# Gate and up products of a SwiGLU in seven half-width products per chunk instead of eight

## The chip, the core and the metric

The kernel runs on one core of a Trainium2 chip. The metric is the device time of one execution in microseconds (us); the profile is one execution on the same chip. The engines are named as the profile names them: PE does the matmuls, PEld loads their weights, DVE is the vector engine, ACT the scalar engine, POOL the GpSimd engine, SP issues the DMAs.

## The reference, cut to what is computed

Four SwiGLU feed-forward networks (FFN 0 to 3 below) stand in a trunk of two layers, one ahead of and one behind each mixer; the mixers are a causal pooling layer and a latent attention layer. T = 512 tokens, D = 1024, F = 2816, all in float32.

```python
def swiglu(u, wg, wu, wd):
    return (jax.nn.silu(u @ wg) * (u @ wu)) @ wd

for l in range(DEPTH):
    h = h + 0.5 * swiglu(rmsnorm(h, ffn_pre_norm[l]), ffn_pre_wg[l], ffn_pre_wu[l], ffn_pre_wd[l])
    u = rmsnorm(h, mix_norm[l])
...
    h = h + 0.5 * swiglu(rmsnorm(h, ffn_post_norm[l]), ffn_post_wg[l], ffn_post_wu[l], ffn_post_wd[l])
...
return rmsnorm(h, final_norm)
```

## The kernel before

The residual h lies transposed in SBUF, as eight tiles h0 to h7 of 128 features by 512 tokens. Float32 precision is kept by splitting every operand into a rounded high part and a low part; `mm3` (L84) makes each product of three matmuls, high by high, high by low and low by high (L86 to L88). The high part of a weight tile is a cast on ACT (L118), the low part a subtraction on DVE (L119); a weight tile is 128 x 1024 (512 KB) and comes by one DMA into the ring `wraw` of four.

F is cut into 22 chunks of 128. In an FFN, `rms` sums the squares over the features with eight pairs of one-column matmuls (`token_sums`, L156), takes the root on DVE (`rsqrt`, twelve small operations, L167 to L174) and `on_all` spreads the result to all partitions (a product on DVE called `diag`, L197, a matmul, L204, a copy on ACT called `rb`). The norm is applied behind the gate and up products, so these can start before it is known: the gained, unnormalised h, split into `gh_hi` and `gh_lo`, is their moving operand.

Chunks 0 and 1 are computed together, k by k as h arrives (96 matmuls). Each further chunk takes 48 matmuls of 512 columns, 24 for the gate and 24 for the up product; `gated` (L280) then multiplies by rb on DVE, takes the silu on ACT, multiplies gate and up on POOL (L287) and splits the product into `mh` and `ml`. The down product runs twice per FFN, behind chunk 10 and behind chunk 21: `down` (L317) sums 11 chunks into a PSUM tile for each of the eight d and DVE adds it to h (L324). In the last FFN d = 6 and 7 of the second time go by halves of the tokens, so that the first half of the output can be finished early.

A tile scheduler orders the instructions of each engine from its own estimates. PSUM has a ring of six tiles `mm` and of two tiles `aux`.

Of the kernel before, what the change touches and what calls it, by code (L numbers as in the profile page):

```python
# [16 lines left out]
P = 128  # L17
T = 512
# [4 lines left out]
NFH = NF // 2  # L23
# [17 lines left out]
def trunk_kernel(  # L41
# [20 lines left out]

    nc = tc.nc
# [11 lines left out]
    def f(ap):  # L75
        return ap.bitcast(F32)
# [7 lines left out]
    def mm3(out, w, x, start, stop):  # L84

        nc.tensor.matmul(out, w[0], x[0], start=start, stop=False)  # L86
        nc.tensor.matmul(out, w[0], x[1], start=False, stop=False)  # L87
        nc.tensor.matmul(out, w[1], x[0], start=False, stop=stop)  # L88
# [11 lines left out]
    more, count = [], [0]  # L100

    def load_w(src, parts=1, loads=1, lo_engines=(nc.vector,), before=None):
# [3 lines left out]
        pools = [wsplit_sb] + more  # L106
        pool = pools[count[0] % len(pools)]
        count[0] += 1
        hi = pool.tile([P, UNIT], F32R, tag="whi", name="whi")
        lo = pool.tile([P, UNIT], F32R, tag="wlo", name="wlo")  # L110
# [16 lines left out]
    room = ExitStack()  # L127
    more.append(room.enter_context(tc.tile_pool(name="wsplit2", bufs=4)))
# [80 lines left out]
    class Norm:  # L209
# [39 lines left out]

        def rb(self, ts=slice(0, T)):  # L250
            return on_all(rms(self.squares, D, (ts.stop - ts.start) // P))
# [23 lines left out]

    def ffn(idx, norm, on_h, first=None, last=False):
        rb = norm.rb()
        with tc.tile_pool(name="mid", bufs=1) as midp, tc.tile_pool(name="act", bufs=2) as actp:

            def gated(j, gate, up):  # L280

                tg = actp.tile([P, T], F32, tag="tg", name="tg")
                tu = actp.tile([P, T], F32, tag="tu", name="tu")
                nc.vector.tensor_tensor(out=tg, in0=gate, in1=rb, op=ALU.mult)  # L284
                nc.scalar.activation(tg, tg, AF.Silu)
                nc.vector.tensor_tensor(out=tu, in0=up, in1=rb, op=ALU.mult)  # L286
                nc.gpsimd.tensor_tensor(out=tu, in0=tu, in1=tg, op=ALU.mult)  # L287
                hi = midp.tile([P, T], F32R, tag=f"mh{j}", name=f"mh{j}")
                lo = midp.tile([P, T], F32R, tag=f"ml{j}", name=f"ml{j}")
                nc.scalar.copy(hi, tu)  # L290
                nc.vector.tensor_tensor(out=lo, in0=tu, in1=f(hi), op=ALU.subtract)  # L291
                return hi, lo

            for half in range(2):
                mid = []
                if half == 0:

                    ps = [mm_tile() for _ in range(4)]
                    for u in range(ND // 2):
                        w = part(first[u] if first is not None else load_w(wfirst[idx, u]), 2, 4, P)  # L300
                        for c in (2 * u, 2 * u + 1):
                            for m in range(4):
                                mm3(ps[m], [x[:, c % 2, m] for x in w], norm.gh[c], c == 0, c == ND - 1)
                    mid += [gated(0, ps[0], ps[1]), gated(1, ps[2], ps[3])]
                for j in range(len(mid), NFH):
                    ps = []
                    for m in range(2):
                        w = part(load_w(wgu[idx, half * NFH + j - 2, m]), ND, P)
                        o = mm_tile()
                        for c in range(ND):  # L310
                            mm3(o, [x[:, c] for x in w], norm.gh[c], c == 0, c == ND - 1)
                        ps.append(o)
                    mid.append(gated(j, *ps))

                units = {}

                def down(d, ts):  # L317
                    o = mm_tile()
                    for j in range(NFH):
                        u, k = divmod(d * NFH + j, 8)  # L320
                        if u not in units:
                            units[u] = part(load_w(wd[idx, half, u]), 8, P)
                        mm3(o[:, ts], [x[:, k] for x in units[u]], [x[:, ts] for x in mid[j]], j == 0, j == NFH - 1)
                    nc.vector.scalar_tensor_tensor(  # L324
                        out=h[d][:, ts], in0=o[:, ts], scalar=0.5, in1=h[d][:, ts], op0=ALU.mult, op1=ALU.add)
                    if half == 1:
                        on_h(d, ts)

                n_whole = ND - 2 if last and half == 1 else ND
                for d in range(n_whole):  # L330
                    down(d, slice(0, T))
                if n_whole < ND:
                    for th in range(2):
                        for d in range(n_whole, ND):
                            down(d, slice(th * T // 2, (th + 1) * T // 2))
# [107 lines left out]
    class Shared:  # L443


        def __init__(self, norm):
            mean = mean_of(token_sums(norm.squares), D)
            self.gh, self.r = norm.gh, on_all(rsqrt(mean, "rms_r"))
            shared_kv(mean, self.r)

        def rb(self):
            return self.r
# [354 lines left out]
```

## Time and profile before

| | us |
|---|---|
| median of 3 runs | 1790.08 (1787.37 to 1966.82) |
| the profiled execution | 1788.47 |
| its span | 1786.7 |
| PE busy | 1758.8 (98%) |
| DVE busy | 843.2 (47%) |
| ACT busy | 629.4 (35%) |
| POOL busy | 316.2 (18%) |

The span is the time from the first to the last instruction that the profiler recorded; the execution's own time is 1.8 us longer. A matmul's recorded duration is longer than its spacing to the next, since matmuls are pipelined: what one costs in a stream is read from start to start. The same holds, by about 0.08 us, for DVE operations that follow each other.

### The profile page before, as it was taken

Reading aid. Unit: us, or ns where it says so; the run is one execution under the profiler, and the core shown is the slowest. Engines: PE = TensorE matmul, PEld = TensorE weight load, DVE = VectorE, ACT = ScalarE, POOL = GpSimd, SP = SyncE. Lnnn points to the kernel's source line nnn. Section 1 sums busy time; section 2 is a strip of 40 time slices with the busy share of each in tenths; the row PEclk is TensorE's granted clock in tenths of the full one; section 3 lists DMA queues with packets and bytes.
Section 4 is the critical chain, followed back from the end, with each engine's and each line's share of the span. In section 5 each row is a group of like instructions: output and inputs, shape, how many; then the busy total and the mean of one; then the engine's idle time right before and its main releaser. Section 6 shows DMA issues by size and latency. Waiting matters only on the chain. (4 is left out here: it accounts for less than half of the span.)

```text
span 1786.7 us, 20848 instructions
## 1 busy us (share of the span) xinstructions
PE 1758.8 (98%) x8238; PEld 1466.5 (82%) x8238; DVE 843.2 (47%) x1248; ACT 629.4 (35%) x948; POOL 316.2 (18%) x192
## 2 busy tenths in 40 slices
PE   8999999999999999999999999999999999999997
PEld 6888888888888888888888888888887888888886
DVE  7443444465433444465434443487675744334433
ACT  5332222353221233333322332376664532222221
POOL 3220022122210121101200222212121222101212
PEclk9999999999999999999999999999999999999998
DMA  7322223222322233223232322221221333222301
GB/s 249 102 98 95 94 96 104 95 85 87 102 95 94 95 100 100 95 87 96 95 96 95 104 95 71 65 69 51 77 84 59 130 100 102 94 95 95 103 27 48
DMA packets 49553, 166.34 MB, mean 93 GB/s; under 512 B 6320, under 2 KB 6320, under 8 KB 49456
## 3 DMA queue, kind: packets, MB, share of 16 engines
q1 hardware_dynamic: 49456, 165.02, 28.3%
q8 instruction: 65, 1.06, 0.3%
q14 instruction: 32, 0.26, 0.0%
HBM read 158.44 MB, written 2.10 MB: 90 GB/s over the span
## 5 line engine op out<-in xcount | busy, mean ns | idle before, releaser
L118 ACT CAST whi<-wraw 128x1024 fp32r<-128x1024 f32 (+2 forms) x332 | 315.4, 959 | 730.8 <-PE mm L87 656.3
L86 PE MATMUL mm<-gh_hi,whi 128*128 128x512 f32 x1424 | 557.2, 391 | 6.6 <-ACT whi L118 6.6
L87 PE MATMUL mm<-gh_lo,whi 128*128 128x512 f32 x1424 | 556.9, 391 | 0.0
L88 PE MATMUL mm<-gh_hi,wlo 128*128 128x512 f32 x1424 | 555.3, 391 | 0.0
L119 DVE TENSOR_TENSOR wlo<-wraw,whi 128x1024 fp32r<-128x1024 f32 (+2 forms) x302 | 372.0, 1233 | 201.2 <-ACT whi L118 200.6
L287 POOL TENSOR_TENSOR tu<-tu,tg 128x512 f32<-128x512 f32 x88 | 192.5, 2188 | 1029.2 <-ACT whi L118 842.7
L86 PEld LDWEIGHTS mm<-gh_hi,whi 128*128 128x128 f32 x1424 | 268.6, 189 | 63.0 <-ACT whi L118 6.6
L88 PEld LDWEIGHTS mm<-gh_hi,wlo 128*128 128x128 f32 x1424 | 268.6, 189 | 56.7 <-issue 0.7
L87 PEld LDWEIGHTS mm<-gh_lo,whi 128*128 128x128 f32 x1424 | 268.7, 189 | 56.3 <-issue 0.5
L86 PE MATMUL mm<-mh,whi 128*128 128x512 f32 (+1 forms) x726 | 277.9, 383 | 0.0
L87 PE MATMUL mm<-ml,whi 128*128 128x512 f32 (+1 forms) x726 | 276.4, 383 | 0.0
L88 PE MATMUL mm<-mh,wlo 128*128 128x512 f32 (+1 forms) x726 | 276.4, 383 | 0.0
L286 DVE TENSOR_TENSOR tu<-mm,rb 128x512 f32<-128x512 f32 x88 | 60.8, 691 | 260.5 <-PE mm L88 260.5
L87 PEld LDWEIGHTS mm<-ml,whi 128*128 128x128 f32 x726 | 136.4, 188 | 26.8
L86 PEld LDWEIGHTS mm<-mh,whi 128*128 128x128 f32 x726 | 136.4, 188 | 26.6
L88 PEld LDWEIGHTS mm<-mh,wlo 128*128 128x128 f32 x726 | 136.4, 188 | 26.5
L291 DVE TENSOR_TENSOR ml<-tu,mh 128x512 fp32r<-128x512 f32 x88 | 63.3, 721 | 131.4 <-ACT mh L290 130.9
L290 ACT CAST mh<-tu 128x512 fp32r<-128x512 f32 x88 | 54.5, 621 | 188.9 <-POOL tu L287 188.2
L324 DVE SCALAR_TENSOR_TENSOR h<-mm,h 128x512 f32<-128x512 f32 (+1 forms) x66 | 44.5, 675 | 143.0 <-PE mm L88 143.0
L284 DVE TENSOR_TENSOR tg<-mm,rb 128x512 f32<-128x512 f32 x88 | 60.8, 691 | 85.7 <-PE mm L88 81.4
L241 POOL TENSOR_TENSOR sq_acc<-sq_acc,sq 128x512 f32<-128x512 f32 (+1 forms) x43 | 60.4, 1405 | 217.7 <-ACT sq L237 217.2
L119 POOL TENSOR_TENSOR wlo<-wraw,whi 128x512 fp32r<-128x512 f32 (+1 forms) x30 | 40.6, 1354 | 195.9 <-ACT whi L118 189.8
(165 smaller groups left out, 1450.4 us busy)
## 6 DMA issues: line engine op xcount, KB each, us to landing
wraw<-in_wgu SPq DMA_DIRECT2D x160, 512.0 KB, 3.3
wraw<-in_wd SPq DMA_DIRECT2D x88, 512.0 KB, 3.3
wraw<-in_wo SPq DMA_DIRECT2D x16, 512.0 KB, 3.4
wraw<-in_wfirst SPq DMA_DIRECT2D x12, 512.0 KB, 3.3
wraw<-in_wheads SPq DMA_DIRECT2D x8, 512.0 KB, 3.3
h<-in_xT SPq DMA_DIRECT2D x8, 256.0 KB, 5.9
wraw<-in_wfirst SPq DMA_DIRECT2D x8, 256.0 KB, 6.0
qr<-yh SPq DMA_DIRECT2D x32, 64.0 KB, 2.0
```

The source lines that it names most:

```text
L86: nc.tensor.matmul(out, w[0], x[0], start=start, stop=False)
L87: nc.tensor.matmul(out, w[0], x[1], start=False, stop=False)
L88: nc.tensor.matmul(out, w[1], x[0], start=False, stop=stop)
L118: nc.scalar.copy(hi[:, s], raw[:, s])
L119: lo_engines[i % len(lo_engines)].tensor_tensor(out=lo[:, s], in0=raw[:, s], in1=f(hi[:, s]), op=ALU.subtract)
L241: nc.gpsimd.tensor_tensor(out=self.acc[:, ts], in0=self.acc[:, ts], in1=self.sq[:, ts], op=ALU.add)
L284: nc.vector.tensor_tensor(out=tg, in0=gate, in1=rb, op=ALU.mult)
L286: nc.vector.tensor_tensor(out=tu, in0=up, in1=rb, op=ALU.mult)
L287: nc.gpsimd.tensor_tensor(out=tu, in0=tu, in1=tg, op=ALU.mult)
L290: nc.scalar.copy(hi, tu)
L291: nc.vector.tensor_tensor(out=lo, in0=tu, in1=f(hi), op=ALU.subtract)
L324: nc.vector.scalar_tensor_tensor(out=h[d][:, ts], in0=o[:, ts], scalar=0.5, in1=h[d][:, ts], op0=ALU.mult, op1=ALU.add)
```

## The change

Chunks 2 to 21 of each FFN compute gate and up by Strassen's algorithm for 2 x 2 blocks. The blocks of the weights are gate and up by the two halves of K; the blocks of the tokens are the two halves of K by the two halves of T. Seven products replace eight, each of 4 k by 3 matmuls of 256 columns: 84 matmuls of 256 columns per chunk in place of 48 of 512. Products p1 to p7 are summed in PSUM and, where they enter more than one result, by ACT copies and DVE sums.

- `group_weights` forms four sums of weight blocks per chunk with POOL additions of 128 x 512 (L165 of the new code) and splits 3.5 tiles of 128 x 1024 (a, half of rb, s13, s24) where the kernel before split two.
- `Quarters` forms the sums of token blocks once per FFN, 24 small DVE operations (those of 256 columns and the splits of `t12`, `t4` and `t3`, L357 to L375) and their casts on ACT.
- The down product goes in six parts of 2, 4, 4, 4, 4 and 4 chunks (`PARTS`). Two d of a part stand behind each chunk of the next part; h is added to six times per d instead of twice (L491).
- The product of gate and up is on DVE rather than POOL.
- PE's order in an FFN is the order of the code (`manual_schedule`): in the first Strassen chunk p1, p2, p6, then `on_all`, then p7 and p5; in a later one p1, p2, p4 of the chunk before, p6, p5, p3 of the chunk before, p7, then the two down products.
- Weight splits have one ring of four pairs; a further ring of four (`wsplit2`, `wsplit3`) is gone, and small pools `wb`, `wf`, `gx` and `act` are new.

```diff
+PARTS = (2, 4, 4, 4, 4, 4)
+    def group_weights(idx, g, wb):
+        ra, rb = (wraw_sb.tile([P, UNIT], F32, tag="wraw", name="wraw") for _ in range(2))
+        nc.sync.dma_start(ra, wgu[idx, g - 2, 0])
+        nc.sync.dma_start(rb, wgu[idx, g - 2, 1])
+        q0, q1, whole = slice(0, 512), slice(512, UNIT), slice(0, UNIT)
+        def add(out, x, y):
+            nc.gpsimd.tensor_tensor(out=out, in0=x, in1=y, op=ALU.add)
+        a = split_w(ra, wsplit_sb, "w")
+        split_into(a, ra, whole)
+        a22 = split_w(rb[:, q0], room.wf, "f")
+        split_into(a22, rb[:, q0], q0)
+        add(rb[:, q0], rb[:, q0], rb[:, q1])
+        add(rb[:, q1], rb[:, q1], ra[:, q0])
+        s13 = split_w(rb, wsplit_sb, "w")
+        split_into(s13, rb, whole)
+        add(ra[:, q0], rb[:, q0], ra[:, q0])
+        add(ra[:, q1], ra[:, q0], ra[:, q1])
+        s24 = split_w(ra, wb, "w")
+        split_into(s24, ra, whole)
...
+            def product(g, to, w, x, start=True):
+                if start:
+                    acc[g][to] = mm_tile()[:, :HT]
+                for k in range(4):
+                    mm3(acc[g][to], weights[g][w](k), quarters.operand(x, k), start and k == 0, k == 3,
+                        skip_group_check=True)
...
+            def p3(g):
+                product(g, "y1", "s4", "b22", start=False)
+                y = acc[g].pop("y1")
+                nc.vector.tensor_tensor(out=y, in0=act[g]["c16"], in1=y, op=ALU.add)
+                gate_half(g, 1, y)
+                gate = act[g]["g"]
+                silu(gate)
+                m = room.act.tile([P, T], F32, tag="m", name="m", bufs=3)
+                nc.vector.tensor_tensor(out=m[:, :HT], in0=acc[g].pop("x"), in1=gate[:, :HT], op=ALU.mult)
+                nc.vector.tensor_tensor(out=m[:, HT:], in0=act[g]["c167"], in1=gate[:, HT:], op=ALU.mult)
+                split_mid(g, m)
...
+                    p1(g)
+                    p2(g)
+                    if before is None:
+                        p6(g)
+                        rb = norm.spread(r)
+                        for j in range(2):
+                            gated(j, ps[2 * j], ps[2 * j + 1])
+                        gate_half(g, 0, acc[g].pop("y2"))
+                        p7(g)
+                        p5(g)
+                        up_half(g)
+                    else:
+                        gate_half(g, 0, acc[g].pop("y2"))
+                        p4(before)
+                        p6(g)
+                        p5(g)
...
+                            p3(before)
+                            p7(g)
+                            up_half(g)
...
+                    if n_part == 0:
+                        todo = [(d, None) for d in ((), (0, 1, 2), (3, 4, 5), (6, 7))[i]]
+                    elif i == 0:
+                        todo = [(d, rest) for d in (0, 1)]
+                    else:
+                        todo = [(d, [n - 1]) for d in (0, 1)] if i == 1 else []
+                        todo += [(2 * i + j, None) for j in range(2)]
```

On PE, the kernel before has `on_all` of FFN 0 (its matmul is L204) among the products of chunks that came ahead of it:

```order
L86 MATMUL mm<-gh_hi,whi 128x512
L87 MATMUL mm<-gh_lo,whi 128x512
L204 MATMUL aux<-diag,ones 128x512
L88 MATMUL mm<-gh_hi,wlo 128x512
L86 MATMUL mm<-gh_hi,whi 128x512
```

In the changed kernel PE has it (L261) behind p6 of chunk 2, with t the summed token blocks:

```order
L91 MATMUL mm<-t_hi,whi 128x256
L92 MATMUL mm<-t_lo,whi 128x256
L93 MATMUL mm<-t_hi,wlo 128x256
L261 MATMUL aux<-diag,ones 128x512
L91 MATMUL mm<-gh_hi,whi 128x256
L92 MATMUL mm<-gh_lo,whi 128x256
```

Ahead of `on_all` of FFN 0 PE now has the token sums, 96 matmuls of 512 columns (chunks 0 and 1) and 36 of 256 (p1, p2 and p6 of chunk 2); before it had the token sums and 110 of 512.

On DVE in FFN 0 before, the last rows ahead of diag are the root's, among weight splits (L119) for chunks ahead:

```order
L172 TENSOR_TENSOR rms_t<-rms_r,mean 128x4
L173 SCALAR_TENSOR_TENSOR rms_t<-rms_t,rms_r 128x4
L119 TENSOR_TENSOR wlo<-wraw,whi 128x1024
L174 SCALAR_TENSOR_TENSOR rms_r<-rms_t,rms_r 128x4
L172 TENSOR_TENSOR rms_t<-rms_r,mean 128x4
L173 SCALAR_TENSOR_TENSOR rms_t<-rms_t,rms_r 128x4
L174 SCALAR_TENSOR_TENSOR rms_r<-rms_t,rms_r 128x4
L197 TENSOR_TENSOR diag<-ident,rms_r 128x512
```

In the changed kernel twelve rows of DVE in the same place begin with the last token sums (t, gh_lo) and the weight splits of chunks 2 and 3 (L153); the root's rows stand between these, and diag (L254) follows eleven rows behind the last one shown:

```order
L362 SCALAR_TENSOR_TENSOR t_416<-h_89,g_neg,t_409 128x256
L375 TENSOR_TENSOR gh_lo<-t_416,gh_hi 128x256
L153 TENSOR_TENSOR wlo<-wraw,whi 128x1024 x2
L375 TENSOR_TENSOR t_lo<-t_409,t_hi 128x512
L239 TENSOR_SCALAR mean<-aux 128x4
L375 TENSOR_TENSOR t_lo<-t_416,t_hi 128x256
L224 TENSOR_SCALAR rms_t<-mean 128x4
L153 TENSOR_TENSOR wlo<-wraw,whi 128x1024
L226 TENSOR_SCALAR rms_r<-rms_t 128x4
L410 TENSOR_TENSOR mm<-c_460,mm 128x256
L153 TENSOR_TENSOR wlo<-wraw,whi 128x1024
L229 TENSOR_TENSOR rms_t<-rms_r,mean 128x4
```

From the first gh_lo to diag DVE has 68 rows in FFN 0, where it had 37; POOL, for which DVE's weight splits wait, has eight additions of weight blocks for these two chunks besides its six sums of squares.

On DVE a chunk in the middle of an FFN was five rows before, two weight splits, tg, tu and ml:

```order
L284 TENSOR_TENSOR tg<-mm,rb 128x512
L119 TENSOR_TENSOR wlo<-wraw,whi 128x1024
L286 TENSOR_TENSOR tu<-mm,rb 128x512
L119 TENSOR_TENSOR wlo<-wraw,whi 128x1024
L291 TENSOR_TENSOR ml_944<-tu,mh_943 128x512
```

It is sixteen rows now, of which twelve stand here; L153 and L119 are weight splits, L410, L432 and L442 sums of products, L416, L455, L447 and L448 the gating, L491 adds to h:

```order
L153 TENSOR_TENSOR flo<-wraw,fhi 128x512
L442 TENSOR_TENSOR mm<-c_1429,mm 128x256
L416 TENSOR_TENSOR gate<-mm,rb 128x256
L153 TENSOR_TENSOR wlo<-wraw,whi 128x1024
L455 TENSOR_TENSOR gate<-gate,rb 128x512
L119 TENSOR_TENSOR wlo<-wraw,whi 128x1024
L432 TENSOR_TENSOR c_1645<-c_1645,mm 128x256
L447 TENSOR_TENSOR m<-mm,gate 128x256
L448 TENSOR_TENSOR m<-c_1479,gate 128x256
L153 TENSOR_TENSOR wlo<-wraw,whi 128x1024
L491 SCALAR_TENSOR_TENSOR h_88<-aux,h_88 128x512
L462 TENSOR_TENSOR ml_1630<-m,mh_1629 128x512
```

The four rows not shown are the split of a, the sum L410, the first half's L416 and the second L491.

## Rows read from the trace of the kernel before

**Rows 1.** Page, part 1: busy us, share of the span and instructions of each engine.
```profile
PE 1758.8 (98%) x8238; PEld 1466.5 (82%) x8238; DVE 843.2 (47%) x1248; ACT 629.4 (35%) x948; POOL 316.2 (18%) x192
```

**Rows 2.** Page, part 5: costliest groups; busy, mean ns | idle before, its releaser.
```profile
L118 ACT CAST whi<-wraw 128x1024 fp32r<-128x1024 f32 (+2 forms) x332 | 315.4, 959 | 730.8 <-PE mm L87 656.3
L86 PE MATMUL mm<-gh_hi,whi 128*128 128x512 f32 x1424 | 557.2, 391 | 6.6 <-ACT whi L118 6.6
```

**Rows 3.** Timeline, PE, 48 matmuls apart: start us, duration us, instruction.
```profile
302.36 0.39 PE L86 MATMUL mm<-gh_hi,whi 128*128 128x512 f32 x1
...
313.24 0.39 PE L86 MATMUL mm<-mh,whi 128*128 128x512 f32 x1
```

**Rows 4.** Timeline, PE, last FFN, 35 matmuls of 256 columns apart.
```profile
1753.95 0.28 PE L86 MATMUL mm<-mh,whi 128*128 128x256 f32 x1
...
1758.15 0.28 PE L88 MATMUL mm<-mh,wlo 128*128 128x256 f32 x1
```

**Rows 5.** Groups by shape, DVE: busy us, mean ns | idle before.
```profile
L264 DVE TENSOR_TENSOR ptl<-aux,pth 128x256 fp32r<-128x256 f32 x16 | 6.7, 416 | 0.6 <-ACT pth L263 0.6
```

**Rows 6.** Timeline, DVE, FFN 0: 128x512 with and without POOL beside it.
```profile
15.97 1.78 DVE L224 SCALAR_TENSOR_TENSOR gh_lo<-h,g_sb,gh_hi 128x512 fp32r<-128x512 f32 x1
17.68 1.78 DVE L119 TENSOR_TENSOR wlo<-wraw,whi 128x512 fp32r<-128x512 f32 x1
19.38 0.74 DVE L224 SCALAR_TENSOR_TENSOR gh_lo<-h,g_sb,gh_hi 128x512 fp32r<-128x512 f32 x1
20.05 0.68 DVE L119 TENSOR_TENSOR wlo<-wraw,whi 128x512 fp32r<-128x512 f32 x1
```

**Rows 7.** Timeline, POOL, FFN 0: one 128x512 addition.
```profile
10.79 1.29 POOL L241 TENSOR_TENSOR sq_acc<-sq_acc,sq 128x512 f32<-128x512 f32 x1 [1.74 <-ACT sq L237]
```

**Rows 8.** Timeline, PE in FFN 0 around the token sums.
```profile
22.05 0.38 PE L156 MATMUL aux<-ones,sq 128*128 128x1 f32 x2 [0.56 <-DVE sq L234]
...
25.49 0.63 PE L87 MATMUL mm<-gh_lo,whi 128*128 128x512 f32 x1
25.91 0.63 PE L88 MATMUL mm<-gh_hi,wlo 128*128 128x512 f32 x1
```

**Rows 9.** Timeline, FFN 0: DVE from its first row to diag, then PE's on_all.
```profile
5.51 0.75 DVE L224 SCALAR_TENSOR_TENSOR gh_lo<-h,g_sb,gh_hi 128x512 fp32r<-128x512 f32 x1 [4.48 <-ACT gh_hi L219]
...
35.94 0.69 DVE L197 TENSOR_TENSOR diag<-ident,rms_r 128x512 f32<-128x512 f32 x1
...
38.07 1.02 PE L204 MATMUL aux<-diag,ones 128*128 128x512 f32 x2
```

**Rows 10.** Timeline, FFN 1: the pooling's h, a weight split, PE's first product.
```profile
389.77 0.74 DVE L385 SCALAR_TENSOR_TENSOR h<-mm,g_sb,h 128x512 f32<-128x512 f32 x1
390.43 1.22 DVE L119 TENSOR_TENSOR wlo<-wraw,whi 128x1024 fp32r<-128x1024 f32 x1
391.56 0.74 DVE L385 SCALAR_TENSOR_TENSOR h<-mm,g_sb,h 128x512 f32<-128x512 f32 x1
...
396.18 0.44 PE L86 MATMUL mm<-gh_hi,whi 128*128 128x512 f32 x1
```

**Rows 11.** Windows, ahead of FFN 3: busy us of PE, PEld, DVE, ACT, POOL, then the clock.
```profile
1392.00:1413.50 21.50, 21.50 (x97) 17.61 (x96) 21.50 (x23) 15.79 (x22) 10.21 (x6) 1.00 0.46 153
```

**Rows 12.** Timeline, DVE, FFN 3: the root's first row and diag.
```profile
1416.20 0.15 DVE L182 TENSOR_SCALAR mean<-aux 128x4 f32<-128x4 f32 x1
...
1418.64 0.69 DVE L197 TENSOR_TENSOR diag<-ident,rms_r 128x512 f32<-128x512 f32 x1
```

**Rows 13.** Page, part 6: a weight tile's DMA, KB and us to landing.
```profile
wraw<-in_wgu SPq DMA_DIRECT2D x160, 512.0 KB, 3.3
```

**Rows 14.** Timeline, the kernel's tail: DVE and POOL.
```profile
1762.60 0.43 DVE L234 TENSOR_TENSOR sq<-h 128x256 f32<-128x256 f32 x1
...
1773.07 5.50 POOL L691 TENSOR_TENSOR y<-hg,rb 128x256 f32<-128x256 f32 x8 [4.06 <-ACT rb L206]
...
1779.40 1.41 DVE L706 TENSOR_SCALAR y<-mm,rms_r 128x512 f32<-128x512 f32 x2
```

More of the change, by code (lines that the diff above doesn't have):

```diff
@@ L22 @@
 NF = F // P
-NFH = NF // 2
+HT = T // 2
+PARTS = (2, 4, 4, 4, 4, 4)
+N_MID = 8
 H = 16
@@ L105, in load_w @@
         raw = wraw_sb.tile([P, UNIT], F32, tag="wraw", name="wraw")
[L106 to L110, printed above, removed]
+        hi = wsplit_sb.tile([P, UNIT], F32R, tag="whi", name="whi")
+        lo = wsplit_sb.tile([P, UNIT], F32R, tag="wlo", name="wlo")
         for i in range(loads):
@@ L248, in add, with r, spread @@
                 step()
+        def r(self, ts=slice(0, T)):
+            return rms(self.squares, D, (ts.stop - ts.start) // P)
+        def spread(self, r):
+            return on_all(r)
         def rb(self, ts=slice(0, T)):
-            return on_all(rms(self.squares, D, (ts.stop - ts.start) // P))
+            return on_all(self.r(ts))
     def split_gain(src, base, c, pool, tag):
@@ L288, in gated @@
                 hi = midp.tile([P, T], F32R, tag=f"mh{j}", name=f"mh{j}")
                 lo = midp.tile([P, T], F32R, tag=f"ml{j}", name=f"ml{j}")
[L290 to L335, printed above, removed]
@@ new lines, in ffn, with down @@
+            blocks, units, o_of = {}, {}, {}
+            whole = slice(0, T)
+            def down(part_of, d, js=None, ts=whole, tile_of=mm_tile):
+                base, n = part_of
+                js = js or range(n)
+                o = o_of.pop(d, None) or tile_of()
+                for j in js:
+                    at = blocks.setdefault((d, base + j), len(blocks))
+                    u, k = divmod(at, 8)
+                    if u not in units:
+                        units[u] = part(load_w(wd[idx, u]), 8, P)
+                    mm3(o[:, ts], [x[:, k] for x in units[u]], [x[:, ts] for x in mids[base + j]], j == 0, j == n - 1)
+                if js[-1] != n - 1:
+                    o_of[d] = o
+                    return
+                nc.vector.scalar_tensor_tensor(
+                    out=h[d][:, ts], in0=o[:, ts], scalar=-0.5, in1=h[d][:, ts], op0=ALU.mult, op1=ALU.add)
+                if base + n == NF:
+                    on_h(d, ts)
@@ L338, in trunk_kernel @@
+            n = PARTS[-1]
+            under = base - n, n
+            for js in (range(n - 1), [n - 1]):
+                for d in range(2):
+                    down(under, d, js)
+            n_whole = ND - 2 if last else ND
+            for d in range(2, n_whole):
+                down(under, d)
+            for th in range(2):
+                for d in range(n_whole, ND):
+                    down(under, d, ts=slice(th * HT, (th + 1) * HT))
     norm = Norm(G_PRE)
@@ L671, in trunk_kernel @@
                     out_proj(dd, [heads[4 * q4 - 4 + k] for k in range(4)], wos, False)
-        for dd in range(ND):
-            if dd % 2 == 0:
-                wos = part(load_w(wo[3, dd // 2], **aw), 2, 4, P)
-            out_proj(dd, [heads[12 + k] for k in range(4)], wos, True)
-    more.append(ctx.enter_context(tc.tile_pool(name="wsplit3", bufs=4)))
+    room.open()
+    for dd in range(ND):
+        if dd % 2 == 0:
+            wos = part(load_w(wo[3, dd // 2], **aw), 2, 4, P)
+        out_proj(dd, [heads[12 + k] for k in range(4)], wos, True)
     norm = nxt
@@ L719, in trunk_kernel @@
     ffn(3, norm, on_h, last=True)
+    room.close()
 def _layout(a):
```

189 lines of the change are left out of this document (163 added, 26 removed).

## The prediction

> **What bounds the kernel now.** I read the page first: PE is busy 98% of the span, DVE 47%, POOL 18% [rows 1]. Then the groups of instructions: the costliest matmul waited 6.6 us in 1786.7, while ACT's weight casts waited 656 us for PE to free their buffers [rows 2]. The weights are ready before PE wants them; nearly every microsecond taken off PE's stream comes off the time, as long as PE is not made to wait. The question is therefore double: what the seven products save on PE, and where DVE and POOL, which get more work, become late. For the second I read the heads of the FFNs, since there DVE is full already: ahead of FFN 3 it is busy 21.50 of 21.50 us [rows 11].
>
> **What PE saves.** 48 matmuls of 512 columns take 313.24 - 302.36 = 10.88 us, 0.2267 each [rows 3]. 35 matmuls of 256 columns lie between 1753.95 and 1758.15, 0.120 each [rows 4]; half the columns cost a little over half the time. A chunk goes from 10.88 to 84 x 0.120 = 10.08 us. That is 0.80 us per chunk, for 20 chunks in 4 FFNs 64 us. The down products keep their count and width. An eighth fewer products would be 1.36 us per chunk; the narrower matmul eats 0.56 of it.
>
> The Trainium skill ("TensorE: Matmul & The Clock Gate", section Back-to-back issue gap) gives an isolated gap of N/2.4 + 2.5 ns, which would be 215.8 and 109.2 ns, and a saving of some 95 us instead. Both rows above lie higher, so the sum goes by the rows.
>
> **What a chunk costs DVE and POOL.** First the price of the two beside each other. Alone, two 128x512 operations on DVE start 0.67 us apart (19.38, 20.05); while POOL adds squares they start 1.71 apart (15.97, 17.68) [rows 6]. A POOL addition of that size lasts 1.29 us alone [rows 7], so it takes some 1.04 us from DVE each time, and the two don't run together when both read SBUF. A DVE operation on PSUM isn't stretched; of 256 columns it lasts 0.42 us [rows 5], some 0.35 in a queue.
>
> A 128x1024 split costs DVE 1.13 us start to start (390.43, 391.56) [rows 10]. Per steady chunk: four such splits (a, s13, s24, a down tile) 4.5 us, three of 512 columns 1.8, one multiplication of 256 0.35, that is 6.7 us on SBUF; four POOL additions at 1.04, 4.2 us; PSUM sums, gating and two additions to h, 3.4 us. All in series 14.3 us. PE's period is 10.08 + 24 x 0.2267 = 15.52 us. So DVE and POOL fit, narrowly. The weights' own loop also fits: rb's DMA 3.3 us [rows 13], then the split of its first half, 1.2, four additions, 4.2, and the cast and the split of s24, 2.2, make 10.9 of 15.52, and the rest is for queueing.
>
> The tightest wait of a steady chunk is the PSUM ring: six tiles, three per chunk, so p1 needs the tile x of two chunks ago, which the gating behind p3 frees. p3 ends six products, 8.64 us, into the chunk; then come a sum and a half gate on DVE (0.7), the silu on ACT and two multiplications (some 2), and ahead of them in DVE's queue a split or two with their POOL share (3 to 3.5): 14.4 to 15.1 us against 15.52. Nothing is lost there, but in the first chunk of a part, where the two down products lack their last chunk, the period is 14.16. I take 0.5 us for each of the four in an FFN, 8 us in all (0 where the splits are not in the way, 16 at 1 us each), and 5 (0 to 8) for the chunk with three-deep down products in the first part.
>
> **The heads.** This is where I expect most of the gain to go. diag and PE's `on_all` stand behind all that DVE has ahead of them in its queue, and that now includes the token sums and the weights of chunks 2 and 3.
>
> FFN 0: 68 DVE rows from the first gh_lo to diag. By size: 7 of 1024 at 1.13, 7.9; 23 of 512 at 0.63, 14.5; 24 of 256 on SBUF at 0.34 (0.43 recorded [rows 14], less the overlap), 8.2; the root's 12 at 0.2, 2.4 (1416.20 to 1418.64 [rows 12]); the rest 1: 34 us. 14 POOL additions at 1.04 add 14.5. From 5.51 [rows 9], with 1.5 us of gaps, diag is done at about 55.5. PE wants it at 37.5: `on_all` stood at 38.07 behind 110 matmuls [rows 9]; 14 fewer of 512 and 36 more of 256 make +1.1, and the slower clock behind the token sums, where PE had been idle 0.56 us [rows 8], may go, -1.7. Stall 18 us; with no POOL share at all it is 4, with all gaps kept 24.
>
> FFN 1: DVE has the pooling's h, the gh_lo, the token sums and the same weights, some 36 us and 12 of POOL, from 389.77 [rows 10]: diag at 438. PE starts at 396.18 [rows 10], and 96 x 0.2267, the token sums 2.2 and 36 x 0.120 bring it to 424.7. Stall 13 (8 to 18). FFN 3: DVE is full [rows 11], and diag was done at 1418.64 + 0.69 [rows 12], but its h comes from the output product, spread over a longer time, and that row of token sums can begin early: 5 (0 to 10). FFN 2 has its rb long before: 1.5 (0 to 6). Sum 37.5.
>
> Behind `on_all` PE goes on with p7 and p5 and then wants p1 of chunk 3, whose tile waits for the gating of chunks 0 and 1: 2 us in each of three heads, 6. After the long gaps the matmuls run at half the clock for a while, as at 25.49 and 25.91, 0.42 apart, behind a gap of only 0.56 us [rows 8]: 2 us at two heads, 4.
>
> **The tail.** From the squares of d = 7, first half, at 1762.60, to the first y of the second half at 1779.40 it took 16.8 us [rows 14]; token sums, root and `on_all` of the first half come to 5.6, POOL's eight outputs 5.5 [rows 14], and the second half's sum of squares, which stands behind them on POOL, 0.7, then token sums and root 3.4: 15.2. But those squares come later with respect to PE's work, since only 24 matmuls of 256 columns remain behind them where 66 did, 42 x 0.120 = 5.0. Cost 3.4 us (0 to 5).
>
> **The sum.** 1788.47 - 64 + 8 + 5 + 37.5 + 6 + 4 + 3.4 = 1788.4, less what overlaps: a head that waits longer gives the weight loop a lead, and the first part's stalls (5) are then covered. I forecast **1784 us**. The profiled execution is 1.6 us below the median of the runs, which is nothing here; a measurement of this kernel tells about 2%, 36 us, from no change.
>
> **Rivals.** *The heads cost little* (faster). If POOL's additions find gaps in DVE's queue, or DVE's order on the chip lets diag through, the heads cost 4 + 4 + 0 + 0 instead of 37.5, the steady chunks nothing, and the tail 3: 1788.5 - 64 + 8 + 6 + 3 = about 1741. For it speaks that ACT and DMA have room; against it, that FFN 3's head is full [rows 11] and that rows 6 show no gap used.
>
> *DVE and POOL set the chunk's period* (slower). 14.3 us of 15.52 leave 1.2. If each addition costs DVE its whole 1.29 us [rows 7], it is 15.3; if the order of the queue also makes DVE wait some 0.5 to 1 us for POOL or ACT in the chain a22, additions, s13, s24, the period is 16.3 to 16.5. The change turns slower by 2% when the period passes 15.52 by 0.5 us in 80 chunks, 40 us beyond the forecast, and at 0.8 to 1 it gives 1848 to 1864, say 1850. For it: the fit is narrow, and two of DVE's weight splits wait for POOL's sums in each chunk. Against it: the loop needs 10.9 of 15.52.
>
> The Trainium skill ("SBUF — State Buffer", section SBUF: two separate sides) speaks for this one: the port pair of the two is an exclusive lock, held for the whole instruction, and the loser blocks fully. Rows 6 and 7 agree that they exclude each other, at 1.04 rather than 1.29 us.
>
> *PE saves nothing at 256 columns* (the change doesn't do what it says). If a stream of 84 with changing weights ran at 0.13 instead of 0.120, a chunk would take 10.92, and the time would be 1788 + 64, about 1850. Rows 4 are such a stream, with a new weight tile every third matmul, so I give this little.
>
> **How the numbers follow.** Forecast 0.46; cheap heads 0.30; DVE and POOL bound 0.20; slow narrow matmuls 0.04. The forecast's own range, from the bounds of heads (12 to 58), chunks (0 to 24) and tail, is 1750 to 1815. With the rivals it is 1738 to 1845: under 1738 stand the heads at nothing and a faster clock, above 1845 half of the slow rivals, together 2 in 10. Faster by over 2% (under 1754) 0.31, slower by over 2% (above 1826) 0.23, the same 0.46.
>
> **What would show it.** In the profile after: PE busy about 1695 us; 256-column matmuls 0.120 apart; PE's idle time ahead of `on_all` 18 us in FFN 0 and 13 in FFN 1, released by diag on DVE; DVE full without a gap from 5.5 to 55 us; POOL's additions (L165) above 1.29 us on average; small waits for DVE ahead of p1 in the first chunk of each part. I am wrong if diag comes before PE wants it, or if PE waits in every chunk.

## The result, and the profile after

The changed kernel took 1819.66 us (median of 4 runs, 1818.72 to 1820.23), the kernel before 1788.72 beside it: 1.0177 times as long, 95% interval 1.0157 to 1.0197. I had forecast 1784, with a range of 1738 to 1845: the time lies in the range, but on the other side of no change. The interval lies clear of 1: the change makes the kernel 1.8% slower. The profiled execution took 1819.67 us. One slow execution of the kernel before, 1966.82 us, is in its median and left out of the ratio.

Part 1 of the page of the changed kernel:

```profile
PE 1724.5 (95%) x11076; PEld 1563.6 (86%) x11076; DVE 1334.3 (73%) x2137; ACT 860.1 (47%) x1412; POOL 593.2 (33%) x424
```

The span is 1817.9 us. PE is busy 34.3 us less than in [rows 1] and idle 93.4 us instead of 27.9, 65.5 more; the difference is the 31.2 us of the spans. So two things have to be explained: why PE waits, and why its busy time fell by 34 and not by the 64 us that the sum gave.

The saving itself is there. These two rows of PE's timeline, in a steady chunk of the changed kernel, are 33 matmuls apart:

```profile
118.15 0.28 PE L92 MATMUL mm<-gh_lo,whi 128*128 128x256 f32 x1
...
122.11 0.28 PE L92 MATMUL mm<-t_lo,fhi 128*128 128x256 f32 x1
```

3.96 / 33 = 0.120 us, as in [rows 4]. Over the whole trace, the intervals between two matmuls of 256 columns with no wait and at a granted clock of 1.00, some 6800, have a median of 0.120 us.

The waits of PE in the changed kernel, by what released them: us in total, times, longest us. In this view of the kernel before only two rows were over 2 us, the first of them the start [rows 2].

```profile
PE aux L91 <- DVE h L491: 18.3, 23, 1.0
PE mm L91 <- ACT c L400: 14.9, 3, 7.3
PE aux L261 <- DVE diag L254: 10.0, 4, 3.0
PE aux L213 <- POOL sq_acc L298: 8.2, 3, 5.0
PE mm L91 <- ACT whi L118: 7.2, 1, 7.2
PE aux L91 <- ACT mh L461: 7.1, 1, 7.1
PE mm L91 <- ACT whi L152: 6.4, 1, 6.4
PE mm L93 <- DVE wlo L153: 6.2, 1, 6.2
PE mm L91 <- DVE pvl L330: 4.3, 1, 4.3
```

The first row is a small wait that comes back 23 times; the others are long ones, two or three in each FFN, besides the start (whi L118), the pooling layer (pvl) and the tail. The places, from PE's timeline: FFN 0 (44.30 to 55.65), FFN 1 (443.79, 449.76), FFN 2 (781.23, 847.38) and FFN 3 (1465.11, 1470.11).

```profile
44.30 0.58 PE L91 MATMUL mm<-t_hi,whi 128*128 128x256 f32 x1 [6.37 <-ACT whi L152]
...
51.25 0.58 PE L93 MATMUL mm<-t_hi,wlo 128*128 128x256 f32 x1 [6.16 <-DVE wlo L153]
...
55.65 1.22 PE L261 MATMUL aux<-diag,ones 128*128 128x512 f32 x1 [1.89 <-DVE diag L254]
...
443.79 0.58 PE L91 MATMUL mm<-t_hi,whi 128*128 128x256 f32 x1 [7.29 <-ACT c L400]
...
449.76 1.22 PE L261 MATMUL aux<-diag,ones 128*128 128x512 f32 x1 [3.04 <-DVE diag L254]
...
781.23 0.37 PE L213 MATMUL aux<-ones,sq_acc 128*128 128x1 f32 x1 [5.03 <-POOL sq_acc L298]
...
847.38 0.79 PE L91 MATMUL aux<-mh,whi 128*128 128x512 f32 x1 [7.09 <-ACT mh L461]
...
1465.11 0.58 PE L91 MATMUL mm<-t_hi,whi 128*128 128x256 f32 x1 [6.24 <-ACT c L400]
...
1470.11 1.22 PE L261 MATMUL aux<-diag,ones 128*128 128x512 f32 x1 [2.08 <-DVE diag L254]
```

In FFN 0 `on_all` comes at 55.65, where it came at 38.07 [rows 9]. The reader should see that PE waits three times on the way there, and that only the last wait names diag: most of the time is spent ahead of p6 and within it, on the high and then the low part of s24, the last of the weight sums.

The small wait stands at the start of each part. DVE and POOL, then PE, in the timeline of the changed kernel around 130 us:

```profile
125.41 4.05 POOL L165 TENSOR_TENSOR wraw<-wraw 128x512 f32<-128x512 f32 x3
...
128.46 1.54 DVE L455 TENSOR_TENSOR gate<-gate,rb 128x512 f32<-128x512 f32 x1 [0.70 <-ACT gate L454]
129.93 0.68 DVE L491 SCALAR_TENSOR_TENSOR h<-aux,h 128x512 f32<-128x512 f32 x1
...
130.66 0.50 PE L91 MATMUL aux<-mh,whi 128*128 128x512 f32 x1 [1.00 <-DVE h L491]
```

PE wants a third aux tile for the down product, of which there are two; the first is free when DVE has added it to h (L491), and DVE comes to that 0.9 us late, since the multiplication ahead of it (L455) takes 1.54 us beside POOL's additions.

### The profile page after: what moved, and what is told of

The parts are those of the page before. It is cut to its first block, busy times and chain, and to the rows that moved or that the text cites. A ratio compares the mean times of both kernels' runs of the same rounds, so it can differ in the third digit from the quotient of the medians.

```text
span 1817.9 us, 28071 instructions
## 1 busy us (share of the span) xinstructions
PE 1724.5 (95%) x11076; PEld 1563.6 (86%) x11076; DVE 1334.3 (73%) x2137; ACT 860.1 (47%) x1412; POOL 593.2 (33%) x424
## 4 chain that ended last, share of the span: by engine, by line
PE 79%; DVE 13%; issue 3%; ACT 2%; DMA 2%; POOL 1%; SPq 0%; POOLq 0%; DVEq 0%; ACTq 0%
PE mm L91 18%; PE mm L93 18%; PE mm L92 18%; PE aux L91 7%; PE aux L92 7%; PE aux L93 6%; DVE gate L455 2%; DVE gh_lo L281 1%; DVE h L491 1%; DVE wlo L153 1%; DVE wlo L119 1%; ACT gate L454 1%; DMA wraw<-in_wgu 1%; PE mm L810 1%; DMA wraw<-in_wfirst 1%
## 5 line engine op out<-in xcount | busy, mean ns | idle before, releaser
L165 POOL TENSOR_TENSOR wraw<-wraw 128x512 f32<-128x512 f32 x320 | 468.7, 1465 | 824.0 <-DVE flo L153 736.7
L91 PE MATMUL mm<-gh_hi,whi 128*128 128x256 f32 (+1 forms) x1424 | 424.3, 298 | 8.6 <-ACT whi L118 7.2
L93 PE MATMUL mm<-gh_hi,wlo 128*128 128x256 f32 (+1 forms) x1424 | 421.3, 296 | 1.0 <-DVE wlo L119 1.0
L92 PE MATMUL mm<-gh_lo,whi 128*128 128x256 f32 (+1 forms) x1424 | 421.1, 296 | 0.0
L152 ACT CAST whi<-wraw 128x1024 fp32r<-128x1024 f32 x240 | 251.7, 1052 | 232.6 <-POOL wraw L165 137.3
L153 DVE TENSOR_TENSOR wlo<-wraw,whi 128x1024 fp32r<-128x1024 f32 x240 | 298.3, 1245 | 5.3 <-ACT whi L152 4.2
L91 PE MATMUL aux<-mh,whi 128*128 128x512 f32 x576 | 228.8, 397 | 25.4 <-DVE h L491 18.3
L92 PE MATMUL aux<-ml,whi 128*128 128x512 f32 x576 | 226.2, 393 | 0.0
L93 PE MATMUL aux<-mh,wlo 128*128 128x512 f32 x576 | 224.9, 391 | 0.0
L91 PE MATMUL mm<-t_hi,whi 128*128 128x256 f32 x640 | 183.2, 286 | 19.9 <-ACT c L400 13.5
L442 DVE TENSOR_TENSOR mm<-c,mm 128x256 f32<-128x256 f32 x80 | 34.3, 429 | 208.8 <-PE mm L93 208.8
L119 DVE TENSOR_TENSOR wlo<-wraw,whi 128x1024 fp32r<-128x1024 f32 (+2 forms) x142 | 160.4, 1130 | 25.8 <-ACT whi L118 25.2
L118 ACT CAST whi<-wraw 128x1024 fp32r<-128x1024 f32 (+2 forms) x172 | 146.1, 866 | 69.5 <-issue 33.7
L455 DVE TENSOR_TENSOR gate<-gate,rb 128x512 f32<-128x512 f32 x88 | 129.2, 1471 | 20.0 <-ACT gate L454 19.9
```

The lines of the kernel that those rows point to most:

```text
L91: nc.tensor.matmul(out, w[0], x[0], start=start, stop=False, **kw)
L92: nc.tensor.matmul(out, w[0], x[1], start=False, stop=False, **kw)
L93: nc.tensor.matmul(out, w[1], x[0], start=False, stop=stop, **kw)
L118: nc.scalar.copy(hi[:, s], raw[:, s])
L119: lo_engines[i % len(lo_engines)].tensor_tensor(out=lo[:, s], in0=raw[:, s], in1=f(hi[:, s]), op=ALU.subtract)
L152: nc.scalar.copy(hi[:, s], raw[:, s])
```

## The experiments

Each edit is made to the changed kernel unless it says otherwise; times in parentheses are differences from 1819.66. A time without an interval is that of a single execution.

**1. The last down product of a part's first two d, earlier.**

```diff
                             p3(before)
+                            if n_part and i == 1:
+                                for d in (0, 1):
+                                    down(under, d, [n - 1], tile_of=aux_tile)
                             p7(g)
...
-                        todo = [(d, [n - 1]) for d in (0, 1)] if i == 1 else []
-                        todo += [(2 * i + j, None) for j in range(2)]
+                        todo = [(2 * i + j, None) for j in range(2)]
```

> The last chunk's share of d = 0 and 1 is put ahead of p7 in the second chunk of each part, so that h is added while PE does p7. Theory (two PSUM tiles for the down products are too few: the third down product of that chunk waits for DVE to read the first): the sixteen gaps of 1.0 us ahead of a down product go, and the time falls by 16 to 19 us, to about 1802. Rival (DVE's queue is full there and PE will wait for it at the next product): the gaps move to p1 or p3 and the time stays within 5 us of 1820.

1802.42 us (-17.2), 1.0083 [1.0066, 1.0100]. The sixteen waits are gone and none has come in their place. The theory holds: the two PSUM tiles were too few only in that one spot, and one product of cover is enough.

**2. No additions on POOL.** `add` does nothing.

```diff
         def add(out, x, y):
-            nc.gpsimd.tensor_tensor(out=out, in0=x, in1=y, op=ALU.add)
+            pass
```

> Leaves out the four POOL additions of weight blocks per chunk, so that the weights of p3, p5, p6 and p7 are the wrong blocks; all splits stay. Theory (the heads are DVE and POOL in turn, some 1.04 us of DVE's time per addition, eight additions ahead of diag): FFN 0, 1 and 3 lose 6 to 9 us less each, the sixteen gaps of 1.0 us stay: 1790 to 1800. Rival (DVE and POOL also cost something in every steady chunk): more than 40 us go, under 1780. Rival (DVE's own operations make the heads long, POOL runs in their gaps): under 8 us go.

1778.42 us (-41). The number is the first rival's, more than 40 us; its cause isn't there, since PE had no wait to lose in the steady chunks beyond the starts of the parts. The heads give about what the theory said: the waits of FFN 0, 1 and 3 fall by 6.6, 5.4 and 7.9 us. `on_all` in FFN 0 comes at 46.7 instead of 55.65, and the wait ahead of it in FFN 3 falls to 0.4. What the theory lacked: the waits for h fall too, from 18.3 to 10.4 us in all, and so do those of FFN 2 and the time at half clock. One row of PE's waits of this run:

```profile
PE aux L91 <- DVE h L491: 10.4, 16, 0.7
```

DVE's groups by shape of this run give the reason for the waits for h:

```profile
L455 DVE TENSOR_TENSOR gate<-gate,rb 128x512 f32<-128x512 f32 x88 | 59.9, 684 | 5.0 <-ACT gate L454 5.0
```

In the changed kernel the same group was stretched by POOL to more than twice that:

```profile
L455 DVE TENSOR_TENSOR gate<-gate,rb 128x512 f32<-128x512 f32 x88 | 129.2, 1471 | 20.0 <-ACT gate L454 19.9
```

Part 1 of the page of this run gives the price of an addition:

```profile
PE 1716.4 (97%) x11076; PEld 1558.6 (88%) x11076; DVE 1243.7 (70%) x2137; ACT 860.4 (48%) x1412; POOL 126.0 (7%) x104
```

DVE does the same 2137 operations and is busy 90.6 us less than in the changed kernel. So the 320 additions lengthen DVE's operations by 0.28 us each on average, not by the 1.04 us of the sum, and 69 of the 90.6 us are L455's. The run takes away the additions' wait in the chain of the weight sums as well as this lengthening, and doesn't separate the two.

**3. No sums of token blocks.** `prepare` isn't called, and t1, t2 and t4 are parts of gh; 28 DVE operations per FFN fall away, the 24 of 256 columns and the four splits of `t12`.

```diff
-            for k in range(4):
-                self.prepare(norm.base, k)
...
+                           "b22": (self.gh[k + 4], 1), "t1": (self.gh[k], 0), "t2": (self.gh[k], 1), "t4": (self.gh[k + 4], 0)}[name]
```

> Leaves out the sums of token blocks and their splits: the seven products take parts of the unsummed tokens. Theory (the heads are set by the sum of DVE's work ahead of diag, of which the 24 operations of 256 columns and 4 splits of 512 are 11 us): FFN 0, 1 and 3 lose 8 to 11 us less each, and the clock some us: 1785 to 1797. Rival (the weights of the first chunk, and ACT's queue behind POOL's additions, set the wait of p6): p6 still waits 6 us or more in each of the three heads, and under 12 us go.

1788.23 us (-31), inside the theory's range. The rest of FFN 0's wait shows a queue that I had not looked at. ACT and then PE in the timeline of this run:

```profile
39.51 1.04 ACT L152 CAST whi<-wraw 128x1024 fp32r<-128x1024 f32 x1 [3.37 <-POOL wraw L165]
40.46 0.36 ACT L396 COPY c<-mm 128x256 f32<-128x256 f32 x1
...
40.88 0.58 PE L91 MATMUL mm<-gh_hi,whi 128*128 128x256 f32 x1 [5.59 <-ACT c L396]
```

p6 may not add to its tile before ACT has copied p1 from it, and that copy is queued on ACT behind a cast that waits 3.4 us for POOL's addition. This is how the sums on POOL reach PE: through ACT's queue as well as DVE's. It is so in FFN 0 alone here, so the rival for three heads falls.

**4. Chunk 2 the old way, as cover.** 24 matmuls of gate and 24 of up, `on_all` after 36 of them, t3 formed behind them; 19 Strassen chunks.

```diff
+            third(0, range(ND))
+            third(1, range(4))
+            rb = norm.spread(r)
+            third(1, range(4, ND))
+            for j in range(2):
+                gated(j, ps[2 * j], ps[2 * j + 1])
+            gated(2, *o2)
+            quarters.finish(norm.base)
```

> Chunk 2 of each FFN goes the old way, 48 matmuls of 512 columns, with on_all among them, and the sum t3 is formed behind it: 19 Strassen chunks. It costs 0.8 us in each FFN on PE. Theory (the heads wait because PE has too little to do until DVE has caught up): the waits of FFN 0, 1 and 3 fall from 15, 10 and 8 us to 5, 0 to 3 and 0 to 3, the clock falls less: the time falls by 20 to 32 us, to 1788 to 1800. Rival (the work is only put off, and p6 of chunk 3 waits instead): the time falls by less than 8 us.

1817.98 us (-1.7), 1.0169 [1.0153, 1.0184]: the rival. The wait is put off to `on_all` and to p7, which wants t3. PE's timeline of this run in FFN 0:

```profile
49.01 1.22 PE L261 MATMUL aux<-diag,ones 128*128 128x512 f32 x1 [7.03 <-DVE diag L254]
...
64.85 0.58 PE L91 MATMUL mm<-gh_hi,whi 128*128 128x256 f32 x1 [5.39 <-ACT gh_hi L379]
```

In this form more cover does not pay. Part of that is my own edit, which puts t3 behind the gating; a form without that was not tried.

**5. The additions on DVE.**

```diff
-            nc.gpsimd.tensor_tensor(out=out, in0=x, in1=y, op=ALU.add)
+            nc.vector.tensor_tensor(out=out, in0=x, in1=y, op=ALU.add)
```

> The four additions of weight blocks per chunk run on DVE instead of POOL. Theory (a POOL addition takes 1.04 us of DVE's time, the same addition on DVE 0.61; the heads are the sum of both queues): eight additions ahead of diag save some 3.5 us in each of FFN 0, 1 and 3, the chain of the sums gets shorter too, and the sixteen gaps of 1.0 us fall to 0.65: the time falls by 12 to 25 us, to 1795 to 1808. Rival (POOL's additions are worth more beside DVE than in its queue; DVE is then full in the steady chunk): PE waits in the steady chunks, and the time rises by 5 us or more.

1792.61 us (-27.1), 1.0027 [1.0014, 1.0041], a little more than the theory gave. DVE does 320 operations more and PE waits less. Part 1 of the page and DVE's groups by shape of this run:

```profile
PE 1718.0 (96%) x11076; PEld 1558.4 (87%) x11076; DVE 1449.5 (81%) x2457; ACT 858.8 (48%) x1412; POOL 126.9 (7%) x104
...
L165 DVE TENSOR_TENSOR wraw<-wraw 128x512 f32<-128x512 f32 x320 | 220.8, 691 | 8.9
...
L455 DVE TENSOR_TENSOR gate<-gate,rb 128x512 f32<-128x512 f32 x88 | 60.0, 684 | 3.8 <-ACT gate L454 3.8
```

An addition takes 0.69 us on DVE where it took 1.47 on POOL, and the operations beside it have their own length again. DVE is busy 115 us more over the whole execution than in the changed kernel, so the additions on POOL did spare it work; they made it late where PE waited. The waits for h (L491) fall from 18.3 to 4.4 us in all, so about half of the gain lies at the starts of the parts, which is more than the theory gave; the waits in the heads of FFN 0, 1 and 3 fall by 7 us together, less than its 10, and those of FFN 2 by 2. Whether the heads gain by the shorter chain of the sums or by DVE's unlengthened operations this run doesn't separate.

**6. The weights of chunk 3 behind diag.** `last_diag` is the instruction that writes diag.

```diff
+                    if g == 3:
+                        with tc.issue_after(last_diag[0].ins):
+                            weights[g] = group_weights(idx, g, wb)
```

> DVE's splits of chunk 3's weights are queued behind diag (and with them POOL's additions, which overwrite what these splits read). Theory (diag is late because DVE does chunk 3's weights, some 9 us with their additions, ahead of it): on_all comes 6 to 9 us earlier in FFN 0, 1 and 3; chunk 3 then waits for its weights for 2 to 4 us of that, and the time falls by 8 to 18 us. Rival (the head is a matter of DVE's and POOL's whole work until chunk 4, whatever the order): p1, p6 or p3 of chunk 3 wait for all that on_all gained, and the time stays within 5 us of 1820.

1815.42 us (-4.2), 1.0144 [1.0125, 1.0164]: the rival. In FFN 0 p6 of chunk 2 waits 4.0 and 1.9 us and `on_all` not at all; but now p6 of chunk 3 waits for its own s24, in all four FFNs. One of these, in PE's timeline of this run:

```profile
60.10 0.58 PE L93 MATMUL mm<-t_hi,wlo 128*128 128x256 f32 x1 [3.97 <-DVE wlo L153]
```

**7. on_all behind p7 and p5.**

```diff
                         p6(g)
+                        p7(g)
+                        acc[g]["y1"] = aux_tile()[:, :HT]
...
                         rb = norm.spread(r)
```

> In the first Strassen chunk p7 and p5 go ahead of on_all, p5 into an aux tile. Theory (PE has 2.9 us more to do before it needs diag, and diag is set by DVE alone): the waits of FFN 0, 1 and 3 shorten by up to 2.9 us each, 6 to 9 us in all. Rival (the waits are for the weights and token sums of p6, not for diag): the wait ahead of on_all falls from 1.9, 3.0 and 2.1 us to nothing, and what follows on_all waits for the gating instead: less than 4 us.

1820.56 us (+0.9): the rival. `on_all` of FFN 0, 1 and 3 no longer waits, but behind it p1 of chunk 3 waits 2.1 us for the gating.

**8. Matmuls in the wait.**

```diff
+                        for _ in range((51, 59, 0, 51)[idx]):
+                            nc.tensor.matmul(spare[:, HT:], weights[g]["a11"](0)[0], norm.gh[4][0][:, :HT],
+                                             start=True, stop=True, skip_group_check=True)
```

> Between p1 and p2 of the first Strassen chunk, in FFN 0, 1 and 3, PE does 51, 59 and 51 matmuls of 256 columns that nobody reads, as long as the waits ahead of p6 (6.4, 7.3 and 6.2 us). Theory (the time behind a long wait is run at half the clock, and this is 9 to 13 us of the change's loss): the matmuls behind the heads are 0.120 and 0.227 us apart again in most places, and the time falls by 4 to 9 us. Rival (the clock falls for other reasons, or the added matmuls delay p6 by more than they warm): within 3 us of 1820, or slower.

1817.56 us (-2.1), 1.0155 [1.0135, 1.0174]: within the rival's 3 us. The wait ahead of p6 is filled (0.6 us left in FFN 0, none in FFN 1 and 3), but the waits behind it stay (6.1 us for s24 in FFN 0), and in FFN 0 the matmuls run at half the clock behind that one. In FFN 1 the clock stays up: it is granted at 1.00 from 434 to 452 us, where it was 0.50 from 439.0 to 452.6 in the changed kernel, and `on_all` comes 37.4 us after the FFN's first product instead of 39.9. Such gains are taken back elsewhere, in FFN 3 for one by a wait for h of 2.1 us in place of 0.6. What the clock alone costs over the kernel was not separated by this run.

**9. Edits 1 and 5 together.**

> Both edits that gained: the early share of d = 0 and 1, and the additions on DVE. Theory (the two costs lie in different places, the starts of the parts and the heads): 1819.7 - 17.2 - 27.1, less 5 us of the shorter part gaps that both remove, 1775 to 1780, which is 0.5 to 0.8% below the kernel before. Rival (DVE is full, and what one edit takes away comes back in the other): 1785 or more.

1789.56 us (-30.1), 1.0003 [0.9993, 1.0012]. Less than the theory by 10 to 15 us, and in the rival's range; but the reason is not a full DVE, the edits remove the same waits. The waits for h are 18.3 us in the changed kernel, 1.9 in run 1, 4.4 in run 5 and 2.0 here. With the additions on DVE the multiplication ahead of h is short, so the aux tile is freed in time, and moving the down product has little left to gain.

**10. And the sums of squares on DVE.**

```diff
         def accumulate(self, c, ts=slice(0, T)):
             if self.sq is not None and c < ND - 1:
-                nc.gpsimd.tensor_tensor(
+                nc.vector.tensor_tensor(
```

> As the run with both edits, and the sums of squares, six per FFN, are on DVE too, so that POOL does next to nothing beside the FFNs. Theory (each POOL addition takes 1.04 us of DVE's time and 0.61 on DVE itself, and the token sums ahead of the second layer's key and value product, which wait 5.0 us, wait for POOL): 6 to 12 us less than with both edits. Rival (DVE is the bound of the heads, and each operation more on it makes them longer): up to 10 us more.

1775.46 us (-44.2), 0.9924 [0.9909, 0.9940], faster than the kernel before. 14.1 us less than run 9 come from some 41 additions, more than the theory's 6 to 12. The token sums ahead of the second layer's keys wait no more for POOL. PE's longest waits of this run:

```profile
PE aux L261 <- DVE diag L254: 14.4, 4, 5.0
PE mm L91 <- ACT whi L118: 7.0, 1, 7.0
PE mm L91 <- ACT whi L152: 6.9, 1, 6.9
PE aux L91 <- ACT mh L461: 5.0, 1, 5.0
```

The row of POOL's sq_acc is gone; what is left, besides the start (L118), is DVE's own work ahead of diag, s24 in FFN 0 and mh in FFN 2.

**11. And the weights of chunk 3 behind diag.** Edits 1, 5, 10 and 6.

> As the run before in this list, and DVE's splits and additions of chunk 3's weights are queued behind diag. Theory (with the additions on DVE the order of its queue is all that sets the head, and half of what on_all gains is kept): 3 to 8 us less than without it. Rival (the work is only put off): within 3 us.

1773.25 us (-46.4), 0.9907 [0.9884, 0.9929]. The fastest of all, but 2.2 us from run 10, with intervals that overlap: the rival can't be told from the theory here.

**12. The kernel before, without POOL.** The product of gate and up and the sums of squares of the kernel before, on DVE.

```diff
-                nc.gpsimd.tensor_tensor(out=tu, in0=tu, in1=tg, op=ALU.mult)
+                nc.vector.tensor_tensor(out=tu, in0=tu, in1=tg, op=ALU.mult)
...
-                nc.gpsimd.tensor_tensor(
+                nc.vector.tensor_tensor(
```

> The kernel before the change, with its two kinds of POOL work beside the FFNs, the product of gate and up and the sums of squares, on DVE. Theory (an operation moved from POOL to DVE pays only where PE waits for DVE, and before the change PE waits for nothing but some 6 us): within 4 us of the kernel before. Rival (POOL's additions slow the kernel before as well): 8 us or more less, so that the gain of the same edit in the changed kernel isn't the change's.

1784.21 us, 0.9984 [0.9970, 0.9998] of the kernel before, that is 3 to 4 us less: the theory, though a small gain is there. So POOL's price is paid mainly where PE waits for DVE, and it was the change that made PE wait. Against this version run 11 is still 11 us faster.

## Why the prediction was wrong, step by step

I sum what PE lost beyond 0.120 and 0.2267 us from matmul to matmul, over all pairs of the two traces: 120 us after, 21 before. The 99 us more, less the 64 saved, make some 35, near the 31.2 of the spans (the tail and the narrow matmuls are not in it). The forecast had 60. At half clock means at a granted clock of 0.50.

| term | forecast | measured |
|---|---|---|
| saved on PE | 64 | 64 |
| FFN 0 | 18 | 15.4 |
| FFN 1 | 13 | 10.3 |
| FFN 3 | 5 | 8.3 |
| FFN 2 | 1.5 | 13.5 |
| starts of parts | 13 | 18.3 |
| behind on_all | 6 | 0 |
| half clock | 4 | 17 |
| pooling, tail | 3.4 | 6 |
| after each wait, and rest | -4 | 10 |

Two steps of the sum failed. FFN 2, put at 1.5 us, cost 13.5. And a wait was priced at little more than its length: the 4 us for half clock, less the 4 us that I took off for overlap, came to nothing, where the two terms cost 27. These make the 39 us that were missing and turned a small gain into a loss. The other terms were each within 6 us and cancel, which is luck in part: the 6 us behind `on_all` did not come, and the starts of parts cost 5 more.

**What PE saves: right.** The formula of the Trainium skill ("TensorE: Matmul & The Clock Gate", section Back-to-back issue gap) gives an isolated gap of 109 ns for 256 columns; the trace does not agree, it has 120 ns again.

**FFN 0, 1 and 3: right in size.** I had diag done in FFN 0 at about 55.5 and PE released at 55.65. These two rows, from DVE's and POOL's timeline of the changed kernel, are the end of the sum that I had made, and six of its additions:

```profile
32.95 10.21 POOL L165 TENSOR_TENSOR wraw<-wraw 128x512 f32<-128x512 f32 x6 [8.29 <-DVE flo L153]
...
54.90 0.69 DVE L254 TENSOR_TENSOR diag<-ident,rms_r 128x512 f32<-128x512 f32 x1
```

From 5.5 to 55.6 us DVE is busy 46.4 of 50.1 us. My sum has 34 us for its operations by themselves, so some 12 us, by this estimate, are what 14 POOL additions cost it, where I had 14.5. Two rows of DVE's timeline show one kind of operation without and with an addition beside it:

```profile
28.39 0.47 DVE L364 SCALAR_TENSOR_TENSOR t<-h,g_sb,b 128x256 f32<-128x256 f32 x1
...
36.30 1.52 DVE L364 SCALAR_TENSOR_TENSOR t<-h,g_sb,b 128x256 f32<-128x256 f32 x1
```

That DVE's and POOL's work ahead of diag sets the heads is shown by runs 2, 3 and 5: less of either, and the heads are shorter. What I did not see is that PE would be stopped at p6 already, by s24 and by ACT's copy; the time to diag covers that, so the size held. Runs 4, 6 and 7 show that the head is a matter of all the work until chunk 3 is under way: whatever one moves behind diag is waited for next.

**FFN 2: a wait put at next to nothing.** I wrote that it has its rb long before: 1.5 us. It has, but the token sums for the shared keys stand at its front and wait 5.03 us for POOL's last sum of squares, 2.10 us long at 779.07 beside DVE's work (run 10 took that wait away); and the down product waits 7.09 us for mh. ACT's timeline shows the second:

```profile
842.84 0.62 ACT L657 CAST ckv<-kvt 128x512 fp32r<-128x512 f32 x1 [0.17 <-DVE kvt L655]
846.71 1.66 ACT L461 CAST mh<-m 128x512 fp32r<-128x512 f32 x3 [3.25 <-DVE ckv L658]
```

The cast of mh starts 3.25 us after its engine is free, behind the keys' normalisation in the queues of DVE and ACT. I read no queue of that FFN and took a missing wait for rb for no wait at all. That the queue is the cause of the second wait is argued from these rows; no run took it away alone.

**Starts of parts: right in size, wrong in place.** 16 waits of 1.0 us and seven of 0.2 to 0.6, in place of 13 us. I had PE wait for the tile x of two chunks ago, and it waits for the third aux tile, because DVE's L455, for which I had 0.6 us, takes 1.47 beside POOL. Run 1 shows it.

**The clock and the rest: the terms most mis-sized.** Behind a long wait the matmuls run at the lower level. In FFN 0 the granted clock is 1.00 up to 43.0 us and 0.50 from 43.1, while PE is still waiting for s24. PE's timeline behind `on_all` of FFN 0, and then where it is back at 2.4 GHz:

```profile
57.73 0.41 PE L92 MATMUL mm<-gh_lo,whi 128*128 128x256 f32 x1
57.95 0.41 PE L93 MATMUL mm<-gh_hi,wlo 128*128 128x256 f32 x1
...
60.23 0.27 PE L92 MATMUL mm<-t_lo,whi 128*128 128x256 f32 x1
60.34 0.28 PE L93 MATMUL mm<-t_hi,wlo 128*128 128x256 f32 x1
```

The window of the first of these, with the columns of [rows 11], has a granted clock of 0.50, that is 1.2 GHz:

```profile
56.70:60.10 3.40, 3.40 (x15) 2.88 (x14) 1.72 (x4) 1.58 (x3) 0.00 (x0) 0.50 0.33 133
```

0.22 us from start to start against 0.11 to 0.12. I took 2 us at two heads; matmuls of 256 and 512 columns at a granted clock of 0.50 lose 20 us over the whole trace, beyond the waits themselves, against 3 before. Behind the start there are eleven waits of over 2 us where there was none. The seven longest, 4.3 to 7.3 us, all have matmuls at 0.50 behind them; the 1.0 us wait at 130.66 has 1.00 behind it. Each wait also costs some 0.16 us beyond its length: that is a matmul's recorded duration less its spacing, 0.28 less 0.120 and 0.39 less 0.2267, the part that its successor would have covered. The 37 waits between such matmuls make 6.5 us; the other 4 us of the term are not explained. The 4 us that I took off for overlap did not exist.

**The rivals.** The slower one had the right cause, DVE and POOL shutting each other out, and the wrong place: in the steady chunk PE doesn't wait. That chunk fits with more room than I had summed. Between 100 and 380 us DVE is busy 206.0 of 280 us, 11.4 in a period of 15.52 where I had 14.3, since an addition costs it 0.28 us on average and not 1.04 (run 2). The cheap heads did not come. The narrow matmuls cost what the rows said. Three sums in the prediction are slightly off and change nothing: FFN 1's terms bring PE to 424.5, not 424.7; the tile x comes at 14.3 to 14.8, not 14.4 to 15.1; and in the slower rival 15.3 with 0.5 to 1 makes 15.8 to 16.3, not 16.3 to 16.5.

The Trainium skill ("SBUF — State Buffer", section SBUF: two separate sides) has the two take an exclusive lock for a whole instruction when DVE has two SBUF inputs. The trace agrees in kind: 1.47 us for L455 beside POOL, 0.68 without it.

## What to carry to other kernels

A change that takes work from the engine that bounds the kernel is paid for where that engine has no lead: here the steady chunk gave all it promised, and four FFNs' long waits and sixteen part starts took it back. Read for each such place every in-order queue between the work added and the engine that waits, ACT's and the copies in it included, and count the long waits as well as their sum, since here the longest had a stretch at half the clock behind them. An operation on POOL spares DVE work on the whole, here 115 us for 320 additions, and still costs time where PE waits for DVE and both read SBUF: it takes longer itself (1.47 against 0.69 us) and can more than double what DVE does beside it. Put on DVE, 320 additions and some 41 sums of squares gave 44 us less together with the earlier down product. The change then beat the kernel before by 0.8%, and by about 0.5% the kernel before with its own POOL work on DVE (run 12).

## What was not expected of the hardware

A DVE operation with two SBUF inputs that runs beside POOL's additions has its whole queue behind it delayed: L455 took 1.47 us on average instead of 0.68, over 88 operations 69 us. On the other operations the additions have little effect in sum: run 2 gives 90.6 us for all of DVE, so 21 us for all other operations together. That DVE with 15% more operations (2457 beside 2137) and 115 us more of busy time left PE waiting less was the largest effect of a single edit that keeps the kernel's result, 27 us.
